# Adding the two halves of a feature block by a transfer instead of by VectorE, in a decoder trunk on one core

## The chip, the cores and the metric

The kernel runs on one core of a Trainium2 chip. The metric is the device time of one execution in microseconds (us). A core has engines that work side by side, each in the order of its own queue: TensorE (PE in the profile, with its weight loads as PEld), VectorE (DVE), ScalarE (ACT), GpSimd (POOL) and SyncE (SP). Transfers are issued from a queue of SP, ACT or POOL and are then moved by 16 DMA engines. An instruction whose input is not there yet holds up everything behind it in its queue.

## The reference

The reference is a decoder trunk of two layers on 256 tokens of width 2048. Each layer is a mixer and then a squared-ReLU MLP, with norms ahead of them and residual sums behind them. The change touches the MLP alone:

```
def squared_relu_mlp(h, w1, w2):
    return jnp.square(jax.nn.relu(h @ w1)) @ w2
...
        x = x + mix
        x = x + squared_relu_mlp(rms_norm(x, norm_mlp[layer]), mlp_w1[layer], mlp_w2[layer])
```

Here `w1` is 2048 x 8192 and `w2` is 8192 x 2048, both in float32.

## The kernel before, in words

**Split numbers.** Every weight tile is loaded as float32 (`load`, line 127, issued from SP, four buffers) and split in two parts (`halves`): ScalarE writes the rounded part `wh` (line 135), VectorE writes the rest, `wl`, as the difference (line 136). A product is then a sum of three (or two) TensorE products of parts. A raw buffer comes free, and SP can issue the next load into it, when its readers on both engines are done.

**Feature blocks.** An MLP runs in four quarters q. A quarter makes 16 blocks of 128 hidden features each. In a block (`steps_feats` with `bank=3`, `mm_feats`) TensorE multiplies the 16 weight tiles of the block with the tokens' tile, whose 512 columns are 256 tokens of the high part and 256 of the low part (line 164), and adds the product of `wl` and the high part to the first 256 columns (line 168). So the PSUM tile `h` has two halves that must be added. All these blocks use one PSUM bank: the next block's first matmul waits until ScalarE has copied the bank out.

**Evacuation.** `evac_h` does it, once per block: ScalarE copies the bank to `bt_h` (line 1027), VectorE adds the halves into `hu` (line 1029), ScalarE takes the ReLU (line 1030) and the square (line 1032 or 1041). For 12 blocks of a quarter (`SEVEN` = 6 pairs) every second block then makes four sums out of the pair's `hp` on VectorE (lines 1043 to 1045) and splits them into `pt` on ScalarE and VectorE (lines 1047, 1048). The other four blocks are split into `ht`.

**What runs between blocks.** The second product (`steps_seven`) is done for pairs by seven products in place of eight. Each pair has a `go_a` and a `go_b`; they load two tiles `wr`, make their sums `ta` and `tb` on VectorE (lines 225 to 228) and split all of these. `woven` puts 12 such steps between 8 blocks. I call 8 blocks with the steps between them a stretch: a quarter has one for its blocks 0 to 7 (steps on the columns 1024 on, of the quarter before) and one for its blocks 8 to 15 (steps on the columns 0 on). Blocks 0 to 7 of the first quarter stand apart and are not woven.

**What sets the order.** The Python order of calls is only the input of a scheduler: it puts each engine's instructions into a queue by data dependences and its own idea of when each is ready, and an instruction may stand in its queue ahead of one that was written earlier. The order shown below is what came out.

Of the kernel before, what the change touches and what calls it, by code (L numbers as in the profile page):

```python
# [9 lines left out]
F32 = mybir.dt.float32  # L10
FR = mybir.dt.float32r
AF = mybir.ActivationFunctionType
OP = mybir.AluOpType

P = 128
S = 256
# [53 lines left out]
def trunk(ctx: ExitStack, tc: tile.TileContext, plan, a, c_first, c_even, c_odd, out):  # L70
    nc = tc.nc
# [23 lines left out]
    def acc(name, bank=None):  # L95

        if bank is None:
            bank = n_a[0] % 4
            n_a[0] += 1
        return pacc.tile([P, 512], F32, name=name, tag=f"acc{bank}", bufs=1)  # L100
# [70 lines left out]
    def steps_tokens(Ts, w, c0, n, evac, kt=2, order=None, name="a", split_first=False):  # L171

        order = list(order if order is not None else range(len(Ts)))
        box = {}
        groups = [order[i:i + kt] for i in range(0, len(order), kt)]
        if split_first:
            groups[:1] = [[k] for k in groups[0]]

        def make(gi, g):
            def go():  # L180
                if gi == 0:
                    box["a"] = [acc(f"{name}{b}") for b in range(NB)]
                hi, lo = weights(w, g[0], len(g), c0, n)
                for j, k in enumerate(g):
                    mm_tokens(box["a"], n, Ts[k], hi[:, j, :], lo[:, j, :],
                              gi == 0 and j == 0, gi == len(groups) - 1 and j == len(g) - 1)
                if gi == len(groups) - 1:
                    evac(box["a"])
            return go

        return [make(gi, g) for gi, g in enumerate(groups)]
# [239 lines left out]
    def weave(main, side):  # L431

        done = 0
        for i, go in enumerate(main):
            go()
            want = (i + 1) * len(side) // max(1, len(main))
            while done < want:
                side[done]()
                done += 1
        for go in side[done:]:  # L440
            go()
# [509 lines left out]
    def finish(H, wq, evac_y, scale, sm):  # L951

        gfs = []
        for i, (o, n, tag, bufs) in enumerate(((0, 1024, "hp", 1), (1024, 512, "bt", 2), (1536, 512, "bt", 2))):
            g = sm.tile([P, n], F32, name=f"gf{i}", tag=tag, bufs=bufs)
            nc.gpsimd.dma_start(g, a["norm_final"][o:o + n].rearrange("(o d) -> o d", o=1).to_broadcast([P, n]))
            gfs.append((o, n, g))

        def gf(lo, hi):
            return next(g[:, lo - o:hi - o] for o, n, g in gfs if o <= lo < o + n)  # L960

        ss = [sm.tile([P, 5], F32, name=f"ss_f{b}") for b in range(NB)]

        def stats(b, i, v):
            nc.scalar.activation(junk[:, :v.shape[-1]], v, AF.Square, accum_out=ss[b][:, i:i + 1])

        def gain(c):
            def go():
                for b in range(NB):
                    nc.vector.tensor_mul(x[b][c], x[b][c], gf(c * 512, (c + 1) * 512))  # L970
            return go

        for c in range(2):
            for b in range(NB):
                stats(b, c, x[b][c])
        weave(steps_tokens(Late(H), wq, 1024, 512, evac_y(2), name="y"), [gain(0), gain(1)])
        for b in range(NB):
            stats(b, 2, x[b][2])

        def add(b, o, ac):  # L980
            nc.vector.scalar_tensor_tensor(x[b][3][:, o:o + 256], ac[:, :256], scale["s"][:, b:b + 1],
                                           x[b][3][:, o:o + 256], OP.mult, OP.add)

        def evac_a(ac):
            for b in range(NB):
                add(b, 0, ac[b])
                stats(b, 3, x[b][3][:, 0:256])
                nc.vector.tensor_mul(x[b][3][:, 0:256], x[b][3][:, 0:256], gf(1536, 1792))

        weave(steps_tokens(Late(H), wq, 1536, 256, evac_a, kt=4, name="y"), [gain(2)])  # L990
        w = [weights(wq, k, 4, 1792, 256) for k in range(0, 16, 4)]
        for b in range(NB):
            ac = acc(f"z{b}")
            for k in range(16):
                hi, lo = (t[:, k % 4, :] for t in w[k // 4])
                mm_three(ac[:, :256], operand(H[k], b), (hi, lo), k == 0, k == 15)
            add(b, 256, ac)
            stats(b, 4, x[b][3][:, 256:])
            t = sm.tile([P, 3], F32, name=f"var_f{b}")
            nc.vector.tensor_reduce(t[:, 0:1], ss[b], mybir.AxisListType.X, OP.add)  # L1000
            nc.vector.tensor_scalar(t[:, 1:2], t[:, 0:1], 1.0 / D, EPS, OP.mult, OP.add)
            nc.gpsimd.tensor_tensor(t[:, 2:3], t[:, 1:2], neg_half[:, :1], OP.pow)
            r = t[:, 2:3]
            rows = slice(b * P, (b + 1) * P)
            for c in (0, 1):
                nc.vector.tensor_scalar(x[b][c], x[b][c], r, None, OP.mult)
                nc.sync.dma_start(out[0, rows, c * 512:(c + 1) * 512], x[b][c])
            nc.vector.scalar_tensor_tensor(x[b][3][:, 256:], x[b][3][:, 256:], r, gf(1792, 2048), OP.mult, OP.mult)
            nc.scalar.activation(x[b][2], x[b][2], AF.Copy, scale=r)
            nc.sync.dma_start(out[0, rows, 1024:1536], x[b][2])  # L1010
            nc.scalar.activation(x[b][3][:, 0:256], x[b][3][:, 0:256], AF.Copy, scale=r)
            nc.sync.dma_start(out[0, rows, 1536:2048], x[b][3])

    def mlp(layer, norm, nxt):
        st = ExitStack()
        sm = st.enter_context(tc.tile_pool(name=f"mlp{layer}", bufs=1))
        X = Late(norm.T)
        scale = {}
        NF = FF // NQ // P

        def evac_h(H):
            def make(c):
                box = {}

                def go(f, ac):
                    t = sm.tile([P, 512], F32, name="bt_h", tag="bt", bufs=2)
                    nc.scalar.activation(t, ac, AF.Copy)
                    u = sm.tile([P, S], F32, name="hu", tag="hu", bufs=2)
                    nc.vector.tensor_add(u, t[:, :S], t[:, S:])  # L1029
                    nc.scalar.activation(u, u, AF.Relu)  # L1030
                    if c >= SEVEN:
                        nc.scalar.activation(u, u, AF.Square)
                        H[2 * c + f] = sm.tile([P, 2, S], FR, name="ht", tag="ht", bufs=2 * (NF // 2 - SEVEN))
                        split_to(H[2 * c + f], u)
                        return
                    if f == 0:
                        box["r"] = sm.tile([P, 8, P], F32, name="hp", tag="hp", bufs=1)
                    r = box["r"]
                    dst = r[:, 1:3, :] if f == 0 else r[:, 0:4:3, :]
                    v = u.rearrange("p (b t) -> p b t", b=NB)  # L1040
                    nc.scalar.activation(dst, v, AF.Square)
                    if f == 1:
                        nc.vector.tensor_tensor(r[:, 4:6, :], r[:, 1:3, :], r[:, 2:4, :], OP.subtract)
                        nc.vector.tensor_tensor(r[:, 6, :], r[:, 5, :], r[:, 1, :], OP.subtract)
                        nc.vector.tensor_tensor(r[:, 7, :], r[:, 0, :], r[:, 6, :], OP.add)
                        pt = sm.tile([P, 2, 8, P], FR, name="pt", tag="pt", bufs=SEVEN)
                        nc.scalar.activation(pt[:, 0], r, AF.Copy)
                        nc.vector.tensor_tensor(pt[:, 1], r, pt[:, 0].bitcast(F32), OP.subtract)
                        H[2 * c], H[2 * c + 1] = (pt, 0), (pt, 1)
                return go  # L1050
            return make
# [32 lines left out]

        def blocks(q, H):

            ev = evac_h(H)

            def block(i):
                def go():  # L1090
                    run(steps_feats(X, ("mlp_w1", layer, 0), q * (FF // NQ) + i * P,
                                    lambda f, ac: ev[i // 2](i % 2, ac), n=P, name="h", kt=8, bank=3))
                return go

            ev = [ev(c) for c in range(NF // 2)]
            return [block(i) for i in range(NF)], ev

        H = [None] * NF
        hs, ev = blocks(0, H)
# [8 lines left out]
        for q in range(NQ):  # L1108
# [16 lines left out]
            H = [None] * NF  # L1125
# [11 lines left out]
    mix, w_out, ev, side, st = even_layer(n0)  # L1137
# [5 lines left out]
    mix, w_out, ev, side, st = odd_layer(n2)  # L1143
# [53 lines left out]
```

## Time and profile before

| what | us |
|---|---|
| three runs | 2128.31, 2131.53, 2126.43 (median 2128.31) |
| the profiled execution's own time | 2125.81 |
| its span, first to last instruction | 2124.0 |
| TensorE busy | 2098.3 |
| VectorE busy | 1727.1 |
| ScalarE busy | 1301.9 |
| GpSimd busy | 6.1 |

TensorE is busy for 99% of the span. Its matmuls are pipelined and their shown durations overlap, so the gaps before its instructions say more than the share: a row of the timeline ends with the idle time of the engine just before the row, and what ended it. The first MLP runs from about 359 to 1050 us, the second from about 1428 to 2112 us.

### The profile page before, as it was taken

The numbers are of one execution on the slowest core, as the hardware profiler recorded it, in microseconds if no ns is written. First come the engines' busy times: TensorE is split into PE (matmuls) and PEld (weight loads), VectorE is DVE, ScalarE is ACT, GpSimd is POOL, SyncE is SP. The second block draws the span as 40 slices with busy tenths as digits, with TensorE's granted clock in tenths as the row PEclk, the third lists the DMA queues.
The fourth block names the chain that finished last, engine by engine and source line by source line (L and its number), as shares of the span: only waits on it lengthen the run. The fifth ranks groups of instructions, "written<-read, shape, count | busy, mean of one in ns | idle before, by whom it ended". The sixth has DMA issues, their size and how long they took to land.

```text
span 2124.0 us, 29506 instructions
## 1 busy us (share of the span) xinstructions
PE 2098.3 (99%) x10953; PEld 1803.9 (85%) x10953; DVE 1727.1 (81%) x2432; ACT 1301.9 (61%) x1871; POOL 6.1 (0%) x13
## 2 busy tenths in 40 slices
PE   9999999999999999999999999999999999999998
PEld 8998888888888888888888888888888888888887
DVE  5678555889999999899877667558899999998985
ACT  6675445766676666667544444557666666666663
POOL 0000000000000000000000000000000000000000
PEclk9999999999999999999999999999999999999999
DMA  8554455556566566565655555555665665665664
GB/s 294 168 175 157 159 178 179 189 185 212 180 210 195 193 199 205 187 211 190 201 190 172 177 177 169 166 182 179 200 195 189 208 198 189 207 197 193 205 216 141
DMA packets 115296, 404.51 MB, mean 190 GB/s; under 512 B 12944, under 2 KB 13584, under 8 KB 115152
## 3 DMA queue, kind: packets, MB, share of 16 engines
q1 hardware_dynamic: 114624, 401.07, 58.0%
q0 software_dynamic: 384, 1.51, 0.3%
q8 instruction: 85, 1.39, 0.3%
q14 instruction: 59, 0.48, 0.1%
q10 hardware_dynamic: 144, 0.06, 0.0%
HBM read 400.49 MB, written 2.10 MB: 190 GB/s over the span
## 4 chain that ended last, share of the span: by engine, by line
PE 67%; DVE 19%; DMA 8%; issue 3%; ACT 2%; DVEq 0%; POOLq 0%; POOL 0%; SPq 0%; ACTq 0%
PE h L164 12%; DVE wl L136 11%; DMA wr<-in_mlp_w 8%; PE h L168 6%; PE k L164 3%; PE o L154 3%; PE o L156 3%; PE o L155 3%; PE q L164 3%; PE yc L154 3%; PE yc L155 3%; PE yc L156 3%; DVE ta L225 2%; PE v L154 2%; PE v L156 2%
## 5 line engine op out<-in xcount | busy, mean ns | idle before, releaser
L136 DVE TENSOR_TENSOR wl<-wr,wh 128x1024 fp32r<-128x1024 f32 (+4 forms) x769 | 865.8, 1136 | 270.4 <-ACT wh L135 264.9
L135 ACT ACTIVATE wh<-wr 128x1024 fp32r<-128x1024 f32 (+4 forms) x769 | 752.7, 987 | 512.9 <-PE h L164 121.0
L164 PE MATMUL h<-T,wh 128*128 128x512 f32 x2048 | 515.1, 392 | 9.9 <-ACT wh L135 7.8
L164 PEld LDWEIGHTS h<-T,wh 128*128 128x128 f32 x2048 | 373.9, 188 | 90.1 <-ACT wh L135 11.6
L168 PEld LDWEIGHTS h<-T,wl 128*128 128x128 f32 x2048 | 279.3, 190 | 20.1
L168 PE MATMUL h<-T,wl 128*128 128x256 f32 x2048 | 285.5, 282 | 0.0
L225 DVE TENSOR_TENSOR ta<-wr,wr 128x1024 f32<-128x1024 f32 x87 | 106.3, 1222 | 46.4 <-DMA wr<-in_mlp_w 46.0
L155 PE MATMUL ym<-wl,pt 128*128 128x512 f32 x348 | 136.7, 393 | 0.0
L156 PE MATMUL ym<-wh,pt 128*128 128x512 f32 x348 | 135.4, 389 | 0.0
L154 PE MATMUL ym<-wh,pt 128*128 128x512 f32 x348 | 135.4, 392 | 0.0
L135 ACT ACTIVATE wh<-ta 128x1024 fp32r<-128x1024 f32 x87 | 92.1, 1059 | 61.4 <-DVE ta L225 60.1
L1030 ACT ACTIVATE hu<-hu 128x256 f32<-128x256 f32 x128 | 52.8, 416 | 106.4 <-DVE hu L1029 106.3
L135 ACT ACTIVATE wh<-tb 128x1024 fp32r<-128x1024 f32 x87 | 91.8, 1056 | 34.2 <-DVE tb L228 34.2
L154 PE MATMUL yc<-wh,pt 128*128 128x512 f32 x285 | 111.3, 390 | 0.0
L155 PE MATMUL yc<-wl,pt 128*128 128x512 f32 x285 | 111.2, 390 | 0.0
L156 PE MATMUL yc<-wh,pt 128*128 128x512 f32 x285 | 110.9, 389 | 0.0
L136 DVE TENSOR_TENSOR wl<-tb,wh 128x1024 fp32r<-128x1024 f32 x87 | 106.1, 1220 | 3.8 <-ACT wh L135 3.3
L136 DVE TENSOR_TENSOR wl<-ta,wh 128x1024 fp32r<-128x1024 f32 x87 | 106.0, 1218 | 0.0
L154 PE MATMUL o<-wh,M 128*128 128x512 f32 x256 | 102.3, 400 | 0.0
L156 PE MATMUL o<-wh,M 128*128 128x512 f32 x256 | 99.8, 390 | 0.0
L155 PE MATMUL o<-wl,M 128*128 128x512 f32 x256 | 99.6, 389 | 0.0
L154 PE MATMUL yc<-wh,ht 128*128 128x512 f32 x240 | 93.6, 390 | 0.0
(314 smaller groups left out, 3405.3 us busy)
## 6 DMA issues: line engine op xcount, KB each, us to landing
wr<-in_mlp_w SPq DMA_DIRECT2D x512, 512.0 KB, 4.1
wr<-in_od_w_qkv SPq DMA_DIRECT2D x96, 512.0 KB, 4.1
wr<-in_ev_w_in SPq DMA_DIRECT2D x32, 512.0 KB, 3.5
wr<-in_ev_w_out SPq DMA_DIRECT2D x32, 512.0 KB, 3.5
wr<-in_od_w_out SPq DMA_DIRECT2D x32, 512.0 KB, 3.4
wr<-in_ev_w_in SPq DMA_DIRECT2D x24, 344.0 KB, 3.0
wr<-in_ev_w_in SPq DMA_DIRECT2D x15, 364.0 KB, 5.8
wr<-in_mla_w_ukv SPq DMA_DIRECT2D x8, 512.0 KB, 3.6
```

Source lines behind the costliest of these rows:

```text
L135: nc.scalar.activation(hi, raw, AF.Copy)
L136: nc.vector.tensor_tensor(lo, raw, hi.bitcast(F32), OP.subtract)
L154: nc.tensor.matmul(ac, xh, hi, start=first, stop=False)
L155: nc.tensor.matmul(ac, xh, lo, start=False, stop=False)
L156: nc.tensor.matmul(ac, xl, hi, start=False, stop=last)
L164: nc.tensor.matmul(acs[f], hi[:, j, f * P:(f + 1) * P], Ts[j].rearrange("p a t -> p (a t)"), start=first and j == 0, stop=False)
L168: nc.tensor.matmul(acs[f][:, :S], lo[:, j, f * P:(f + 1) * P], Ts[j][:, 0, :], start=False, stop=last and j == n - 1)
L225: nc.vector.tensor_tensor(ta, r0, r1[:, 0:1, :].to_broadcast([P, 2, 512]), OP.add)
L1030: nc.scalar.activation(u, u, AF.Relu)
```

## The change

The tile of the copied bank now takes the sum too: the two halves are added into its first 256 columns. In 12 of 16 blocks of a quarter (those with `i % 8 < 6`; in the first quarter only blocks 8 to 13) the sum is made by a transfer from SBUF to SBUF that adds to its destination and is issued from POOL. In the other blocks VectorE makes it, as before. The rest of a block's evacuation (`rest`: ReLU, square, sums, splits) is kept in `held` and called in the evacuation of the next block, behind that block's copy and add; where VectorE made the sum it is called at once. The tag `bt` has three buffers of 512 columns in place of two, and the tag `hu` (two of 256) is gone.

```
-        def evac_h(H):
+        held = []
+
+        def evac_h(H, by_dma):
             def make(c):
                 box = {}
 
                 def go(f, ac):
-                    t = sm.tile([P, 512], F32, name="bt_h", tag="bt", bufs=2)
-                    nc.scalar.activation(t, ac, AF.Copy)
-                    u = sm.tile([P, S], F32, name="hu", tag="hu", bufs=2)
-                    nc.vector.tensor_add(u, t[:, :S], t[:, S:])
+                    u = sm.tile([P, 512], F32, name="bt_h", tag="bt", bufs=3)
+                    nc.scalar.activation(u, ac, AF.Copy)
+                    if 2 * c + f in by_dma:
+                        nc.gpsimd.dma_start(u[:, :S], u[:, S:], accum_op=OP.add)
+                    else:
+                        nc.vector.tensor_add(u[:, :S], u[:, :S], u[:, S:])
+                    for g in held:
+                        g()
+                    held[:] = [lambda: rest(f, u[:, :S])]
+                    if 2 * c + f not in by_dma:
+                        held.pop()()
+
+                def rest(f, u):
                     nc.scalar.activation(u, u, AF.Relu)
...
-            ev = evac_h(H)
+            ev = evac_h(H, [i for i in range(NF) if i % 8 < 6 and (q or i >= 8)])
```

In ScalarE's queue before, where the first MLP's third quarter begins (blocks 0 and 1; L1027 is the copy of the bank, L1030 the ReLU, L1041 the square, L135 a weight's rounded part):

```order
L1027 ACTIVATE bt_h_6525<-h0_6480 128x512
L1030 ACTIVATE hu_6527<-hu_6527 128x256
L1041 ACTIVATE hp_6530<-hu_6527 128x256
L135 ACTIVATE wh562_6641<-wr559_6635 128x1024
L135 ACTIVATE wh563_6646<-ta561_6639 128x1024
L135 ACTIVATE wh565_6656<-wr560_6637 128x512
L1027 ACTIVATE bt_h_6611<-h0_6566 128x512
L135 ACTIVATE wh564_6652<-tb561_6640 128x1024
L1030 ACTIVATE hu_6613<-hu_6613 128x256
L1041 ACTIVATE hp_6530<-hu_6613 128x2x128
```

The same place in ScalarE's queue now (L1031 is the copy, L1043 the ReLU, L1054 the square, L1060 the split of `hp`):

```order
L1031 ACTIVATE bt_h_6493<-h0_6448 128x512
L1043 ACTIVATE bt_h_6493<-bt_h_6493 128x256
L135 ACTIVATE wh562_6599<-wr559_6593 128x1024
L1054 ACTIVATE hp_6579<-bt_h_6493 128x256
L135 ACTIVATE wh563_6604<-ta561_6597 128x1024
L135 ACTIVATE wh564_6610<-tb561_6598 128x1024
L135 ACTIVATE wh565_6614<-wr560_6595 128x512
L1031 ACTIVATE bt_h_6575<-h0_6530 128x512
L135 ACTIVATE wh567_6630<-wr566_6628 128x1024
L135 ACTIVATE wh569_6652<-wr568_6650 128x1024
L1043 ACTIVATE bt_h_6575<-bt_h_6575 128x256
L1054 ACTIVATE hp_6579<-bt_h_6575 128x2x128
```

Although `rest` is called a block later, the ReLU of a block stands right behind the copy of its own block, or behind two splits of weights, and not behind the copy of the next block.

In ScalarE's queue before, at the blocks 3 and 4 of the same stretch:

```order
L1027 ACTIVATE bt_h_6778<-h0_6733 128x512
L1030 ACTIVATE hu_6780<-hu_6780 128x256
L1041 ACTIVATE hp_6719<-hu_6780 128x2x128
L135 ACTIVATE wh589_6899<-ta587_6892 128x1024
L135 ACTIVATE wh588_6894<-wr585_6888 128x1024
L1047 ACTIVATE pt_6787<-hp_6719 128x1024
L135 ACTIVATE wh590_6905<-tb587_6893 128x1024
L135 ACTIVATE wh591_6909<-wr586_6890 128x512
L135 ACTIVATE wh593_6925<-wr592_6923 128x1024
L135 ACTIVATE wh595_6947<-wr594_6945 128x1024
L1027 ACTIVATE bt_h_6881<-h0_6836 128x512
```

The same place in ScalarE's queue now:

```order
L1031 ACTIVATE bt_h_6740<-h0_6695 128x512
L135 ACTIVATE wh589_6859<-ta587_6852 128x1024
L1043 ACTIVATE bt_h_6740<-bt_h_6740 128x256
L1054 ACTIVATE hp_6744<-bt_h_6740 128x2x128
L135 ACTIVATE wh588_6854<-wr585_6848 128x1024
L135 ACTIVATE wh590_6865<-tb587_6853 128x1024
L135 ACTIVATE wh591_6869<-wr586_6850 128x512
L135 ACTIVATE wh593_6885<-wr592_6883 128x1024
L1060 ACTIVATE pt_6845<-hp_6744 128x1024
L135 ACTIVATE wh595_6907<-wr594_6905 128x1024
L1031 ACTIVATE bt_h_6837<-h0_6792 128x512
```

One split of a weight (wh589) has moved ahead of the ReLU; all others stand behind it. Of the 84 blocks whose halves a transfer adds, 8 have no split between copy and ReLU, 33 have one, 35 two and 8 three.

## Rows read from the trace of the kernel before

**Rows 1.** The page: the span, and each engine's busy time, share and instructions.
```profile
span 2124.0 us, 29506 instructions
...
PE 2098.3 (99%) x10953; PEld 1803.9 (85%) x10953; DVE 1727.1 (81%) x2432; ACT 1301.9 (61%) x1871; POOL 6.1 (0%) x13
```
**Rows 2.** A 50-us window, busy us (instructions): PE, PEld, DVE, ACT, POOL; clock, DMA share, GB/s.
```profile
700.00:750.00 50.00, 48.66 (x243) 40.72 (x242) 47.90 (x62) 32.88 (x42) 0.00 (x0) 1.00 0.54 180
```
**Rows 3.** Waits of TensorE's matmuls, whole span: us in total, times, longest.
```profile
PE h L164 <- ACT wh L135: 7.8, 9, 1.4
...
PE h L164 <- ACT bt_h L1027: 1.9, 6, 0.4
```
**Rows 4.** Groups by line and shape: count, busy us, mean ns, idle before.
```profile
L135 ACT ACTIVATE wh<-wr 128x1024 fp32r<-128x1024 f32 x629 | 661.4, 1056 | 454.3 <-PE h L164 115.0 <-PE o L156 71.8 <-issue 62.1
...
L1027 ACT ACTIVATE bt_h<-h 128x512 f32<-128x512 f32 x128 | 73.8, 583 | 6.1 <-PE h L168 6.1
...
L135 ACT ACTIVATE wh<-wr 128x512 fp32r<-128x512 f32 x91 | 56.8, 624 | 34.3 <-PE yc L156 13.8 <-DMA wr<-in_mlp_w 9.1 <-PE h L164 5.9
...
L1029 DVE TENSOR_TENSOR hu<-bt_h 128x256 f32<-128x256 f32 x128 | 53.0, 419 | 2.3 <-ACT bt_h L1027 2.2
L1030 ACT ACTIVATE hu<-hu 128x256 f32<-128x256 f32 x128 | 52.8, 416 | 106.4 <-DVE hu L1029 106.3
L1047 ACT ACTIVATE pt<-hp 128x1024 fp32r<-128x1024 f32 x48 | 50.7, 1056 | 12.0 <-DVE hp L1045 12.0
...
L1041 ACT ACTIVATE hp<-hu 128x256 f32<-128x256 f32 x96 | 38.9, 411 | 1.8
```
**Rows 5.** The timeline of ScalarE in a stretch of the third quarter: start, us, instruction, idle.
```profile
669.18 0.58 ACT L1027 ACTIVATE bt_h<-h 128x512 f32<-128x512 f32 x1
...
676.19 0.60 ACT L1027 ACTIVATE bt_h<-h 128x512 f32<-128x512 f32 x1 [0.32 <-PE h L168]
...
697.93 0.42 ACT L1030 ACTIVATE hu<-hu 128x256 f32<-128x256 f32 x1 [1.85 <-DVE hu L1029]
...
700.67 1.06 ACT L135 ACTIVATE wh<-ta 128x1024 fp32r<-128x1024 f32 x1 [1.88 <-DVE ta L225]
...
704.59 2.51 ACT L135 ACTIVATE wh<-wr 128x512 fp32r<-128x512 f32 x3
707.01 0.57 ACT L1027 ACTIVATE bt_h<-h 128x512 f32<-128x512 f32 x1
```
**Rows 6.** The timeline of TensorE in the same stretch.
```profile
707.63 2.14 PE L164 MATMUL h<-T,wh 128*128 128x512 f32 x8 [0.42 <-ACT bt_h L1027]
...
719.21 2.14 PE L164 MATMUL h<-T,wh 128*128 128x512 f32 x8 [0.93 <-ACT wh L135]
```
**Rows 7.** The timeline of VectorE: the sums of a pair.
```profile
679.42 0.42 DVE L1043 TENSOR_TENSOR hp<-hp 128x256 f32<-128x256 f32 x1
679.87 0.29 DVE L1044 TENSOR_TENSOR hp<-hp 128x128 f32<-128x128 f32 x1
```
**Rows 8.** DMA issues: queue, count, KB each, median us from issue to landing.
```profile
wr<-in_mlp_w SPq DMA_DIRECT2D x512, 512.0 KB, 4.1
...
out<-x SPq DMA_DIRECT2D x8, 256.0 KB, 2.7
...
gf<-in_norm_final POOLq DMA_DIRECT2D x2, 256.0 KB, 5.1
...
x<-in_x_t SPq DMA_DIRECT2D x2, 128.0 KB, 3.1
```
**Rows 9.** The tile gf, loaded by three transfers from POOL's queue.
```profile
L956 POOL DMA_DIRECT2D gf<-in_norm_final x3: 536/536/583, 2031.5 to 2061.3; - x3
...
DMA to landing us min/median/max: 4.5/5.5/5.7
```
**Rows 10.** The chain that ended last, 655 to 725 us: loads on it.
```profile
667.89 4.34 DMA wr<-in_mlp_w
...
707.75 3.50 DMA wr<-in_mlp_w
```

More of the change, by code (lines that the diff above doesn't have):

```diff
@@ L953, in finish @@
         gfs = []
-        for i, (o, n, tag, bufs) in enumerate(((0, 1024, "hp", 1), (1024, 512, "bt", 2), (1536, 512, "bt", 2))):
+        for i, (o, n, tag, bufs) in enumerate(((0, 1024, "hp", 1), (1024, 512, "bt", 3), (1536, 512, "bt", 3))):
             g = sm.tile([P, n], F32, name=f"gf{i}", tag=tag, bufs=bufs)
```

## The prediction

> **What bounds the kernel now.** I read the page first: TensorE is busy for 2098.3 of 2124.0 us [rows 1]. That share is no room by itself, so I went to the waits of TensorE: in the feature blocks of the MLPs its matmuls waited 7.8 us for rounded weights from ScalarE and 1.9 us for the PSUM bank that ScalarE copies out, 9.7 us together [rows 3]. This is all that the change can give back there. Then the busy time inside an MLP: in 50 us VectorE is busy for 47.9 and ScalarE for 32.9 [rows 2]. VectorE is nearly as full as TensorE, ScalarE has 17 us in 50 free. Last, the timelines of one stretch. The bank's next user, the first matmul of block 5, waited 0.42 us for the copy of block 4, and block 6 waited 0.93 us for a rounded weight [rows 6]; the copy of block 4 itself began only at 707.01, behind splits that had waited 1.88 us for a sum of VectorE, and behind a ReLU that had waited 1.85 us for the add of the halves [rows 5]. So TensorE sets the time, and ScalarE and VectorE are only just in time at the end of a stretch. A delay of ScalarE of more than a microsecond or two late in a stretch is a stop of TensorE.
>
> **What is removed.** Of 128 adds on VectorE, at 419 ns each [rows 4], 84 go (6 in each of 14 stretches): 84 x 0.419 = 35.2 us of busy time, 2.5 us in a stretch. ScalarE's wait for the add goes with them: 106.3 us over 128 ReLUs [rows 4], 0.83 us each. Neither is on TensorE's path but through the 9.7 us above, so the gain is at most 9.7 us, and I book all of it, since a stop by the new wait stands in the place of the old stops.
>
> **What is added.** 84 transfers of 128 KB from POOL's queue, and 84 waits of a ReLU on ScalarE for them. POOL has 6.1 us of work in all [rows 1], so the issue, 0.54 us for a transfer of this queue [rows 9], costs none of the other engines anything; only the last two of them stand behind the first load of `gf`, which waits for the last reader of a buffer. I cost that at nothing, since ScalarE's splits cover a wait of a microsecond there, and at most at one more landing, about 4 us, if they don't.
>
> Call L the time from the end of the copy to the sum being in place. No row of before has an adding transfer, so I bound L: the quickest landing of any large transfer is 2.7 us (256 KB, from SP's queue), the slowest of POOL's queue 5.7 us [rows 8, 9]. Two rows are near: 128 KB from SP's queue, the right size, 3.1 us, and 256 KB from POOL's queue, the right queue, 5.1 us [rows 8]. I take their middle, 4.1 us. The ends 2.7 and 5.7 are kept for the range.
>
> **What stands behind the wait.** In its queue the ReLU stands behind the copy of its own block with none to three splits between, not behind the next block's copy. While it waits, the rounded weights behind it are not made, nor is the next copy, and TensorE waits for both. VectorE then has only the work whose inputs are already there.
>
> I follow ScalarE from the copy of block 0 to that of block 4, with the durations of [rows 4]: copy 0.58, ReLU 0.42, square 0.41, a weight split 1.06 (or 0.62 for a half tile), a `pt` split 1.06. What stands between a ReLU and the next copy, and so cannot overlap the transfer: block 0, ReLU, square, three splits and a half one, copy, 5.2 us; block 1, ReLU, square, the three sums of VectorE (0.42, 0.29 and 0.29 us [rows 7] for the last two of one shape), `pt`, two splits, copy, 5.6 us; block 2 as block 0, 5.2 us; block 3, ReLU, square, four splits and a half one, `pt`, copy, 7.3 us. That is 23.3 us. ScalarE's instructions overlap a little: half, whole and whole split are 2.74 us by their means, and the next instruction began 2.42 us after their start [rows 5], so at the least it is 0.9 times as much, 21 us. I take 22.2 us.
>
> The copy of block 0 ended at 669.18 + 0.58 = 669.76, and block 5 could have begun at 707.63 - 0.42 = 707.21 [rows 5, 6]. That leaves 37.45 us for four landings and 22.2 us of work: (37.45 - 22.2) / 4 = 3.81 us. Up to L = 3.8 us TensorE sees nothing. Beyond it, four waits in a row add up, as nothing between them gives time back, and TensorE stops for S = 4 x (L - 3.81) us in a stretch. Blocks 6 and 7 keep the add on VectorE, and there ScalarE catches up, so I count each of the 14 stretches for itself. At L = 4.1 us, S is 1.2 us, and 14 x 1.2 = 16.2 us.
>
> **The sum.** -9.7 + 16.2 = +6.5 us on the profiled execution's 2125.81 us: 2132.3 us. The runs' median, 2128.31, is 2.5 us above that execution, so I forecast 2134.8, rounded 2135 us. It is a narrow balance: the two terms meet at L = 3.98 us, and each 0.1 us of L is 5.6 us.
>
> **A rule of the skill.** The trace has POOL's transfers landing 4.5 to 5.7 us after their issue, for 256 and 512 KB [rows 9]. The Trainium skill's page "DMA: Bandwidth & Descriptors", section "Anatomy of one DMA — SWDGE (gpsimd) path", gives such a transfer a fixed cost of about 2.0 us and 436 KB per further microsecond; for 128 KB that is an estimate of 2.3 us, and for the 256 KB of the trace 2.6 us where the rows have 5.1. By the rule L would be under 3.8 us and the first rival below would hold; the trace's queue, beside the weights' loads, does not bear it out.
>
> **Rivals.**
> 1. *The landing is hidden.* If L is under about 3.8 us (all rows of before load from or store to HBM, and a transfer inside SBUF may be quicker, which speaks for it; the slow rows of POOL's queue speak against it), no stop is added, and VectorE's 2.5 us a stretch shorten what came late there. Half of the 9.7 us comes back, 2125.8 - 4.9 + 2.5 = 2123.4 us; all of it would be 2118.6. Chance 0.38, of which some is within the bound of no change, since the square and the splits now stand behind a split that waits for `ta`.
> 2. *The waits add up badly.* The same chain as the forecast, but with L as POOL's own rows have it, 5.1 us: S = 5.2 us, 14 x 5.2 = 72 us, less 9.7: 2125.8 + 62.5 + 2.5 = 2191 us. It decides from L = 4.8 us on. An adding transfer also has to read its destination, which speaks for it. Chance 0.15.
> 3. *The loads are late.* The weights' loads lie on the chain that ended last, four of them in 70 us, of 3.5 to 5.2 us [rows 10], the first and the last of the four. An adding transfer moves a quarter of a load's 512 KB, by its 4.1 us [rows 8] about 1.0 us of the engines. If two of the four loads in a stretch are each held up by it, 14 x 2 = 28 us, less the 9.7: 2125.8 + 18.3 + 2.5 = 2146.6 us, slower, whatever L is. Against it: the DMA engines have a share of 0.54 only [rows 2]. Chance 0.10.
>
> **How the numbers follow.** The forecast with L between about 3.8 and 4.8 us has 0.37. What a measurement can tell from no change is 0.2%, 4.3 us. Slower by more: rivals 2 and 3, and of the forecast's cases those above L = 4.06 us, some 0.22: together 0.47. Faster by more: most of rival 1, 0.30. No change gets the rest, 0.23. The range: below it ends a little under the case in which all 9.7 us come back (2118.6), at 2117; above it goes to L = 4.8 us, S = 4.0 us, 14 x 4.0 - 9.7 = 46 us, 2125.8 + 46 + 2.5 = 2174 us. The likeliest case alone spans 2119 to 2174 as well, as its L does; the end at L = 5.7 us (S = 7.6 us, +97 us) is left out.
>
> **What would show it.** In the profile after: 84 fewer adds on VectorE and some 35 us less busy time there; 84 transfers on POOL's queue whose median landing is 4 us or a little less, counted from the issue; ScalarE's ReLU waiting for that transfer 1 to 3 us in most blocks (0.83 us before); and TensorE waiting in the feature blocks for the copy of the bank (L1031) and for `wh`, about 16 us in place of 9.7, most of it at blocks 4 to 6 of a stretch. I am wrong if the transfers land in under 3.5 us and these waits of TensorE shrink, or if TensorE stops for the loads of weights instead.

## The result, and the profile after

The changed kernel takes 2232.01 us (median, 2228.53 to 2239.33) beside 2128.82 us of the kernel before on the same chip: 1.0493 times as long, 95% interval 1.0475 to 1.0511. The prediction said 2135 us with a range to 2174. Slower was right; the size, 103 us in place of 6.5, was not.

The page's first lines, to lay beside [rows 1]:

```profile
span 2237.6 us, 29744 instructions
PE 2142.7 (96%) x10953; PEld 1813.2 (81%) x10953; DVE 1710.2 (76%) x2348; ACT 1282.7 (57%) x1871; POOL 79.0 (4%) x97
```

TensorE is busy for 96% of the span in place of 99%, and its busy time itself grew by 44 us with the same number of matmuls. TensorE's waits, after [rows 3] (engine, line that waited, releaser: total us, times, longest):

```profile
PE h L164 <- ACT bt_h L1031: 37.5, 21, 2.9
PE ym L155 <- DVE wl L136: 20.5, 31, 1.0
PE h L164 <- ACT wh L135: 10.4, 12, 2.1
PE ym L154 <- ACT wh L135: 5.6, 9, 0.7
...
PE yc L155 <- DVE wl L136: 4.2, 9, 0.7
```

They are 78.2 us in 82 stops where the prediction had 9.7 us to lose or win. In the feature blocks (the rows of `h`, 47.9 us) most of it, 37.5 us, is for the PSUM bank, which ScalarE copies out late; the rows of `ym` and `yc` are the second product's waits for parts of weights. ScalarE's groups by line and shape, after [rows 4], show why:

```profile
L135 ACT ACTIVATE wh<-ta 128x1024 fp32r<-128x1024 f32 x87 | 91.9, 1057 | 119.0 <-DVE ta L225 118.8
L1031 ACT ACTIVATE bt_h<-h 128x512 f32<-128x512 f32 x128 | 73.1, 578 | 0.0
L1043 ACT ACTIVATE bt_h<-bt_h 128x256 f32<-128x256 f32 x128 | 52.9, 417 | 258.8 <-DMA bt_h<-bt_h 207.9 <-DVE bt_h L1035 50.8
```

The ReLU (L1043) waited 207.9 us for the transfers, and 106.3 us for VectorE's adds before [rows 4]. The transfers on POOL's queue, and their landing beside that of the weights' loads (KB each, median us from issue to landing), answer to [rows 8]:

```profile
wr<-in_mlp_w SPq DMA_DIRECT2D x512, 512.0 KB, 4.3
bt_h<-bt_h POOLq DMA_DIRECT2D x84, 128.0 KB, 5.2
```

In ScalarE's timeline the first block of a stretch looks like this; its place in the kernel before is the first row of [rows 5] (start, us, what, idle before):

```profile
692.56 1.05 ACT L135 ACTIVATE wh<-wr 128x1024 fp32r<-128x1024 f32 x1
693.52 0.58 ACT L1031 ACTIVATE bt_h<-h 128x512 f32<-128x512 f32 x1
699.25 0.42 ACT L1043 ACTIVATE bt_h<-bt_h 128x256 f32<-128x256 f32 x1 [5.16 <-DMA bt_h<-bt_h]
699.57 1.04 ACT L135 ACTIVATE wh<-wr 128x1024 fp32r<-128x1024 f32 x1
```

Copy and ReLU are neighbours in the queue, so ScalarE does nothing for the whole landing, 5.15 us from the copy's end. That is one of the quicker landings at this place: over the 14 first blocks the mean is 6.3 us. What that does to TensorE, and to its clock, is best seen late in another stretch. TensorE's timeline around the copy of block 4:

```profile
829.45 0.39 PE L156 MATMUL ym<-wh,pt 128*128 128x512 f32 x1
832.57 3.20 PE L164 MATMUL h<-T,wh 128*128 128x512 f32 x8 [2.73 <-ACT bt_h L1031]
835.57 1.62 PE L168 MATMUL h<-T,wl 128*128 128x256 f32 x8
837.02 1.98 PE L164 MATMUL h<-T,wh 128*128 128x512 f32 x8
```

And the same time in windows of 2 us (mind the numbers behind POOL: granted clock, share of the DMA engines, GB/s):

```profile
828.00:830.00 2.00, 1.84 (x9) 1.16 (x7) 2.00 (x5) 0.93 (x1) 0.00 (x0) 1.00 0.71 215
830.00:832.00 2.00, 0.00 (x0) 0.00 (x0) 1.95 (x2) 1.97 (x3) 0.00 (x0) 1.00 0.71 217
832.00:834.00 2.00, 1.43 (x5) 1.14 (x6) 1.86 (x3) 0.52 (x2) 0.87 (x1) 0.82 0.83 270
834.00:836.00 2.00, 2.00 (x8) 1.62 (x7) 1.93 (x3) 1.06 (x1) 0.00 (x0) 0.50 0.98 202
836.00:838.00 2.00, 2.00 (x12) 1.84 (x12) 1.43 (x2) 0.00 (x0) 0.00 (x0) 0.83 0.64 218
```

TensorE stood for 2.73 us; then the granted clock fell to 0.50, the lower of its two levels, and eight matmuls took 3.20 us where eight alike took 1.98 us a moment later. The mean granted clock of the span is 0.989, of before 0.999: 0.011 x 2237.6 - 0.001 x 2124.0 = 22 us of full-speed work not done, or a little less, since TensorE also stood for parts of the slow stretches.

Earlier in the same stretch the clock fell behind shorter stops: there TensorE's listed waits were of 0.74 and 0.78 us, with TensorE busy for 0.96 of 2 us in the window ahead:

```profile
796.00:798.00 2.00, 0.96 (x3) 0.48 (x3) 2.00 (x3) 1.28 (x3) 0.42 (x1) 1.00 0.00 0
798.00:800.00 2.00, 1.61 (x5) 1.01 (x5) 1.53 (x3) 1.03 (x2) 0.45 (x1) 0.79 0.69 212
800.00:802.00 2.00, 1.24 (x3) 0.83 (x3) 1.94 (x2) 1.97 (x4) 0.00 (x0) 0.50 1.05 281
```

So of the profiled span's growth of 113.6 us, 68.5 us are TensorE's listed waits (78.2 less 9.7). A stop costs more than its row lists: from 829.45 to 832.57 there are 3.12 us, of which a matmul needs 0.23 us, so 2.89 us were lost where the row lists 2.73 us. Counted in this way from start to start, the 82 stops cost 93.2 us, and the 15 before cost 12.1 us for their 9.7: another 12.6 us. Matmuls at the lower clock outside these stops took 19 us more, and the rest, some 12 us, lies in gaps too short for the list, most of them ahead of `ym` and `yc`.

### The profile page after: what moved, and what is told of

Same layout as the page of the kernel before. It is cut to its first block, busy times and chain, and to the rows that moved or that the text cites. A ratio compares the mean times of both kernels' runs of the same rounds, so it can differ in the third digit from the quotient of the medians.

```text
span 2237.6 us, 29744 instructions
## 1 busy us (share of the span) xinstructions
PE 2142.7 (96%) x10953; PEld 1813.2 (81%) x10953; DVE 1710.2 (76%) x2348; ACT 1282.7 (57%) x1871; POOL 79.0 (4%) x97
## 3 DMA queue, kind: packets, MB, share of 16 engines
q0 software_dynamic: 12480, 12.52, 3.5%
## 4 chain that ended last, share of the span: by engine, by line
PE 42%; issue 41%; DMA 8%; DVE 4%; ACT 3%; POOL 2%; POOLq 0%; DVEq 0%; ACTq 0%; SPq 0%
DMA bt_h<-bt_h 7%; PE h L164 3%; PE k L164 3%; PE o L156 3%; PE o L154 3%; PE o L155 3%; PE q L164 3%; PE v L154 2%; PE v L156 2%; PE v L155 2%; POOL bt_h L1033 2%; ACT wh L135 2%; DVE wl L136 2%; PE h L168 2%; PE k L168 1%
## 5 line engine op out<-in xcount | busy, mean ns | idle before, releaser
L135 ACT ACTIVATE wh<-wr 128x1024 fp32r<-128x1024 f32 (+4 forms) x769 | 749.4, 984 | 410.9 <-PE o L156 71.8
L164 PE MATMUL h<-T,wh 128*128 128x512 f32 x2048 | 529.8, 401 | 48.0 <-ACT bt_h L1031 37.5
L164 PEld LDWEIGHTS h<-T,wh 128*128 128x128 f32 x2048 | 379.6, 192 | 138.7 <-ACT bt_h L1031 48.5
L168 PEld LDWEIGHTS h<-T,wl 128*128 128x128 f32 x2048 | 284.6, 194 | 21.1
L1043 ACT ACTIVATE bt_h<-bt_h 128x256 f32<-128x256 f32 x128 | 52.9, 417 | 258.8 <-DMA bt_h<-bt_h 207.9
L155 PE MATMUL ym<-wl,pt 128*128 128x512 f32 x348 | 142.1, 408 | 20.6 <-DVE wl L136 20.5
L135 ACT ACTIVATE wh<-ta 128x1024 fp32r<-128x1024 f32 x87 | 91.9, 1057 | 119.0 <-DVE ta L225 118.8
L225 DVE TENSOR_TENSOR ta<-wr,wr 128x1024 f32<-128x1024 f32 x87 | 106.4, 1223 | 46.9 <-DMA wr<-in_mlp_w 46.6
L1033 POOL DMA_DIRECT2D bt_h<-bt_h x84 | 73.0, 869 | 1936.1 <-ACT bt_h L1031 1491.9
L135 ACT ACTIVATE wh<-tb 128x1024 fp32r<-128x1024 f32 x87 | 91.5, 1052 | 45.9 <-DVE tb L228 45.9
L155 PEld LDWEIGHTS ym<-wl,pt 128*128 128x128 f32 x348 | 65.9, 189 | 46.3 <-DVE wl L136 37.3
```

Of the source, the lines that this page charges most:

```text
L135: nc.scalar.activation(hi, raw, AF.Copy)
L155: nc.tensor.matmul(ac, xh, lo, start=False, stop=False)
L164: nc.tensor.matmul(acs[f], hi[:, j, f * P:(f + 1) * P], Ts[j].rearrange("p a t -> p (a t)"), start=first and j == 0, stop=False)
L168: nc.tensor.matmul(acs[f][:, :S], lo[:, j, f * P:(f + 1) * P], Ts[j][:, 0, :], start=False, stop=last and j == n - 1)
L225: nc.vector.tensor_tensor(ta, r0, r1[:, 0:1, :].to_broadcast([P, 2, 512]), OP.add)
L1033: nc.gpsimd.dma_start(u[:, :S], u[:, S:], accum_op=OP.add)
```

## The experiments

Each was timed beside the kernel before on one chip: 2129.11 us for the first four, 2128.61 for the next four, 2128.78 for the last three. A stretch is 8 blocks, 14 stretches have transfers, and the diffs are against the changed kernel unless said otherwise.

**The rest of the evacuation really behind the next block's copy.**

```
-                    nc.scalar.activation(u, ac, AF.Copy)
+                    copy = nc.scalar.activation(u, ac, AF.Copy)
...
                     for g in held:
-                        g()
+                        with tc.issue_after(copy.ins):
+                            g()
```

> As after, but the ReLU of a block whose halves a transfer adds is really queued behind the next block's copy on ScalarE (an order edge, no other edit). Theory A (the loss is ScalarE standing at the ReLU for a landing of 5.2 us with weight splits and the next copy behind it): the next copy comes 7 to 10 us later, so the landing is hidden; ScalarE's wait for these transfers falls from 208 to under 20 us, TensorE's waits in the feature blocks from 48 to 12 us or less, TensorE's clock stays at its full level, time 2117 to 2135 us. Theory B (the transfers hold up the loads of weights, or the chip's transfers cost time wherever the ReLU stands): TensorE or VectorE still waits for loads, 2155 us or more.

Measured: 2138.11 us, 1.0044 [1.0029, 1.0059]. The 84 transfers are as before (landing 5.2 us), no ReLU waits for one, and 94 of the 103 us are gone. What is left of TensorE's waits has nothing in a feature block:

```profile
PE ym L155 <- DVE wl L136: 10.4, 11, 1.8
PE ym L154 <- ACT wh L135: 7.3, 7, 1.7
```

So nearly all of the loss is the place of the ReLU in ScalarE's queue, not the transfers' traffic. But the kernel is still 9 us slower than before, just above what I expected.

**Transfers that nobody waits for.** VectorE adds the halves in every block, the rest is called at once, and the transfers go into a scratch tile, set to zero once, that is not read.

```
-                        nc.gpsimd.dma_start(u[:, :S], u[:, S:], accum_op=OP.add)
-                    else:
-                        nc.vector.tensor_add(u[:, :S], u[:, :S], u[:, S:])
+                        nc.gpsimd.dma_start(junk[:, S:], u[:, S:], accum_op=OP.add)
+                    nc.vector.tensor_add(u[:, :S], u[:, :S], u[:, S:])
...
-                    if 2 * c + f not in by_dma:
-                        held.pop()()
+                    held.pop()()
```

> VectorE adds the halves in all blocks, in place, and ScalarE's ReLU follows at once as in the kernel before; beside it the same 84 adding transfers of 128 KB run from POOL, into a tile that nobody reads. Theory A: 2122 to 2140 us, transfers landing in about 5 us without anybody waiting. Theory B (the transfers themselves cost the time, through the loads of weights): 2150 to 2230 us, weight loads landing clearly later than 4.1 us.

Measured: 2136.55 us, 1.0030 [1.0017, 1.0043]: by the ratio the transfers alone cost 6.4 us (3.6 to 9.2). VectorE's group of `ta` (busy us, mean ns, idle before) shows where:

```profile
L225 DVE TENSOR_TENSOR ta<-wr,wr 128x1024 f32<-128x1024 f32 x87 | 106.4, 1224 | 64.7 <-DMA wr<-in_mlp_w 64.6
```

It waited 64.6 us for loads of weights, and 46.0 us in the kernel before.

**Without the adds.** This one is the kernel before; in the 84 blocks the ReLU reads the first half alone, so the product with the low part of the tokens is left out there.

```
-                    nc.vector.tensor_add(u, t[:, :S], t[:, S:])
-                    nc.scalar.activation(u, u, AF.Relu)
+                    if 2 * c + f in chosen:
+                        nc.scalar.activation(u, t[:, :S], AF.Relu)
+                    else:
+                        nc.vector.tensor_add(u, t[:, :S], t[:, S:])
+                        nc.scalar.activation(u, u, AF.Relu)
```

> The kernel before, with the add of the halves left out in the same 84 blocks (the ReLU reads the first half alone, so the product of the tokens' low part is missing there). It shows what VectorE's relief is worth when nothing takes its place. Theory A: TensorE sets the time and waits only 9.7 us, so 2118 to 2129 us. Rival (VectorE bounds the MLPs): its 35 us come back, 2094 us.

Measured: 2125.14 us, 0.9984 [0.9974, 0.9993]. By the ratio, all that the removal of 84 adds can give is about 3.4 us (1.5 to 5.5).

**Every second transfer.** Blocks 0, 2 and 4 of a stretch, 42 transfers.

```
-            ev = evac_h(H, [i for i in range(NF) if i % 8 < 6 and (q or i >= 8)])
+            ev = evac_h(H, [i for i in range(NF) if i % 8 in (0, 2, 4) and (q or i >= 8)])
```

> As after, but only every second of these blocks (the 1st, 3rd and 5th of a stretch) has a transfer, 42 in all; VectorE adds the others. Theory A with waits that add up along a stretch: between the copies of blocks 0 and 4 two landings of 5.2 us and two waits of 0.83 us stand beside 22.2 us of work, 34.3 of the 37.45 us there, so TensorE hardly stops: 2119 to 2140 us. Rival (each transfer costs the same by itself, 103 us over 84): 2129 + 42 x 1.23 = 2180 us.

Measured: 2215.16 us, 1.0395 [1.0373, 1.0418]. Both numbers fell: half the transfers keep 83% of the loss (86 of 103 us). That broke the prediction's chain, in which two landings would have drawn on the room of four, and made me look at single blocks. In the table, "growth" is worked out from ScalarE's timeline: the time from the start of one block's copy to the next one's, less the same in the kernel before, summed over the 14 stretches (a copy that is moved in its queue shows with opposite signs in two neighbours). "Wait" is the idle time of the ReLU of that block for its transfer, summed likewise.

| us, sums over 14 stretches | 0→1 | 1→2 | 2→3 | 3→4 | 4→5 | 5→6 | 6→7 |
|---|---|---|---|---|---|---|---|
| one interval before, mean | 7.3 | 10.4 | 8.7 | 10.7 | 8.3 | 9.9 | 8.3 |
| changed kernel: splits ahead of the ReLU | 0 or 1 | 2 or 3 | 2 | 1 | 1 (once 2) | 2 | - |
| changed kernel: wait | 80.9 | 15.2 | 17.2 | 20.3 | 22.7 | 51.6 | - |
| changed kernel: growth | 45.4 | -2.6 | 10.2 | 36.1 | 16.1 | 7.0 | -15.3 |
| every second: wait | 80.2 | - | 4.8 | - | 89.8 | - | - |
| every second: growth | 44.3 | -1.2 | 4.9 | 4.4 | 43.9 | -6.4 | 0.0 |
| only block 0: wait | 80.8 | - | - | - | - | - | - |
| only block 0: growth | 46.2 | 0.3 | 10.0 | 2.8 | -1.9 | 2.9 | -0.4 |
| blocks 1 and 2: wait | - | 28.5 | 16.2 | - | - | - | - |
| blocks 1 and 2: growth | 0.3 | 6.6 | 5.7 | -5.1 | 6.5 | -4.6 | -0.1 |
| block 0 held back: wait | 0.4 | 15.7 | 14.8 | 14.7 | 23.8 | 51.3 | - |
| block 0 held back: growth | 4.0 | -1.9 | 5.4 | 35.3 | 17.0 | 8.4 | -19.1 |
| 0, 3 and 4 held back: growth | 2.9 | -2.1 | 4.6 | -8.8 | 28.6 | 2.7 | -12.5 |

With every second block, the growth stands at 0→1 and 4→5 alone: the two blocks whose ReLU comes right behind the copy, or at block 0 in 6 of 14 cases behind one split. Block 2, with two splits between, waits and loses next to nothing. My new theory was that each block has a room of its own.

**Only block 0 of a stretch**, 14 transfers (`i % 8 == 0` in the same line).

> Only block 0 of each of the 14 stretches is summed by a transfer; its ReLU stands right behind its copy (8 of 14) or behind one split (6 of 14). If each landing that no split covers stops TensorE by itself (28 such waits cost 86 us in the kernel with every second block, 3.1 us each), 14 of them cost 35 to 45 us: about 2165 us, 2155 to 2178, with TensorE waiting at block 1 of a stretch for the copy of block 0 or for wh. If waits matter only when four of them add up over a stretch (the chain of the prediction), one of 5 us is far under the 15 us of room: 2122 to 2134 us. If each transfer costs the same wherever it is (86 us over 42), 14 cost 29: about 2157 us.

Measured: 2190.35 us, 1.0294 [1.0277, 1.0311]. 14 transfers cost 62 us, 4.4 us each, more than any theory had. The additive chain (2122 to 2134) is refuted: one wait of 5.8 us in a stretch is not swallowed by the 15 us of room that the sum saw. TensorE stops later than expected: of its 36.7 us of waits in the feature blocks 22.1 us come before block 2 and 11.3 us before block 6. The windows of the stretch with the second longest wait (7.31 us) show something else as well:

```profile
688.00:690.00 2.00, 2.00 (x14) 1.78 (x13) 1.75 (x2) 0.00 (x0) 0.00 (x0) 1.00 1.02 316
690.00:692.00 2.00, 2.00 (x15) 1.79 (x14) 0.86 (x2) 0.00 (x0) 0.00 (x0) 1.00 0.20 68
692.00:694.00 2.00, 2.00 (x10) 1.68 (x9) 0.01 (x1) 1.41 (x3) 0.00 (x0) 1.00 0.04 17
694.00:696.00 2.00, 1.38 (x6) 0.67 (x5) 1.97 (x2) 2.00 (x3) 0.00 (x0) 1.00 0.00 0
```

ScalarE waited here until 692.59. VectorE ran out of rounded weights, SP waited 8.0 us for VectorE to free a raw buffer and issued no load from 686.8 to 695.25, and from 690 to 696 us the DMA engines were nearly idle. The loads behind them come later for it: the wait stops the weights' loads too.

**Only blocks 1 and 2**, 28 transfers, with two or three splits between copy and ReLU (`i % 8 in (1, 2)`).

> Blocks 1 and 2 of each stretch are summed by a transfer, 28 in all; between the copy and its ReLU stand three splits (14 times) or two (14 times). If only uncovered landings cost, ScalarE's waits for the transfers are under 25 us together and the time is 2126 to 2136 us (28 transfers' own cost of about 2 us, less a little of VectorE's relief). If each transfer costs the same wherever it is (2.05 us), 28 cost 57: about 2186 us. The chain of the prediction gives 2122 to 2134 us here as well.

Measured: 2135.26 us, 1.0039 [1.0025, 1.0052]. Twice the transfers of the last run, and a tenth to an eighth of its cost. The ReLU's idle time there:

```profile
  DVE bt_h L1035: 109.0, 90
  DMA bt_h<-bt_h: 44.7, 24
```

44.7 us of waits, more than the 25 expected, cost 6.7 us by the medians (8.3 by the ratio), traffic included; 80.8 us at block 0 cost 62. It isn't the number of transfers nor the sum of the waits, but the block in which a wait falls.

**The rest called at once**, with the transfers (`held.pop()()` without its `if`).

> As the changed kernel, but the rest of the evacuation is called at once and not a block later. If the deferral does nothing, because the scheduler puts the ReLU back behind the copy of its own block anyway (here with 0, 1 or 2 splits between in 10, 45 and 29 of 84 blocks, there 0 to 3 in 8, 33, 35 and 8), the time is the changed kernel's or a little more: 2225 to 2260 us. If the deferral as it stands hides a good part of the landings, its absence costs at least 40 us more: 2270 us or above.

Measured: 2266.51 us, 1.0659 [1.0640, 1.0677], between the two expectations. The deferral as the scheduler took it is worth 34 us, though no ReLU stands behind the next copy: the one of block 5, for instance, waited 69.7 us without it and 51.6 us with it.

**The deferral alone.** VectorE adds in every block, and the rest of the 84 stands behind the next copy.

```
-                    nc.scalar.activation(u, ac, AF.Copy)
-                    if 2 * c + f in by_dma:
-                        nc.gpsimd.dma_start(u[:, :S], u[:, S:], accum_op=OP.add)
-                    else:
-                        nc.vector.tensor_add(u[:, :S], u[:, :S], u[:, S:])
+                    copy = nc.scalar.activation(u, ac, AF.Copy)
+                    nc.vector.tensor_add(u[:, :S], u[:, :S], u[:, S:])
                     for g in held:
-                        g()
+                        with tc.issue_after(copy.ins):
+                            g()
```

> No transfers: VectorE adds the halves in every block; the ReLU of the 84 blocks stands behind the next block's copy (held there). If the 10 us that remained in the kernel with the same order and the transfers come from the transfers' load on the DMA engines, this one is not slower than before: 2118 to 2129 us, since ScalarE no longer waits 0.83 us for each add. If they come from the deferral (the pair's sums and splits come a block later), it stays at about 2134 to 2140 us.

Measured: 2130.08 us, 1.0010 [1.0001, 1.0020], a microsecond above the first range. Deferring alone costs about 2 us, at most 4, and gains nothing: the 0.83 us that ScalarE waited per add were already hidden. The other 7 of the first experiment's 9 us are about the traffic's 6.4; `ta` waited 64.2 us for loads there.

**Block 0 alone held behind the next copy.**

```
                     for g in held:
-                        g()
+                        if (2 * c + f - 1) % 8 == 0:
+                            with tc.issue_after(copy.ins):
+                                g()
+                        else:
+                            g()
```

> As the changed kernel, but the ReLU of block 0 of each stretch really stands behind the copy of block 1 (14 of the 84; the others stand where they stood, with one to three splits in front). In the changed kernel the way from copy to copy has grown, over 14 stretches, by 45 us from block 0 to 1, by 36 from 3 to 4 and by 16 from 4 to 5. If each block has only its own room, and block 0 the least, those 45 us go and nothing else does: about 2187 us, 2176 to 2198. If four waits draw on one pool of 15 us in a stretch (the chain of the prediction), three landings of 5.15 us fit into it: 2128 to 2145 us. If a fixed half of ScalarE's wait is lost (208 us of waits for 104), 81 us of wait go with block 0: about 2192 us.

Measured: 2194.15 us, 1.0310 [1.0293, 1.0327]: 38 us gone. In the table the growth at 0→1 falls from 45.4 to 4.0 and 3→4, 4→5 keep 35.3 and 17.0. With three landings left the pooled chain would have had next to no loss. This run doesn't tell "own room" from "half of each wait"; the 28 transfers at blocks 1 and 2 do.

**Blocks 0, 3 and 4 held back** (`in (0, 3, 4)` in that condition).

> As before, but the ReLUs of blocks 0, 3 and 4 stand behind the next copy (42 of 84); blocks 1, 2 and 5 stay behind their own copies with two to four splits in front. If each block has its own room, 45 + 36 + 16 us go: 2132 to 2150 us, with at most 10 us more of TensorE's waits than in the kernel with all 84 held back (2138). If a fixed half of ScalarE's wait is lost, 124 us of 208 go: about 2170 us. The pooled chain gives 2128 to 2140 us here.

Measured: 2154.81 us, 1.0132 [1.0108, 1.0155], between the two expectations. 3→4 and 4→5 together fall from 52 to 20 us and no further. ScalarE's longest waits there are for something else:

```profile
ACT wh L135 <- DVE ta L225: 147.3, 66, 5.4
...
ACT bt_h L1047 <- DMA bt_h<-bt_h: 66.0, 41, 4.1
```

147.3 us for `ta`, more than twice the 63.1 of the kernel before, and VectorE's `ta` itself waited 71.9 us for loads (46.0 before). Which order of ScalarE's queue makes these loads late was not tried.

**A quarter of the bytes.** The transfers that nobody waits for, with 64 of 256 columns.

```
-                        nc.gpsimd.dma_start(junk[:, S:], u[:, S:], accum_op=OP.add)
+                        nc.gpsimd.dma_start(junk[:, S:S + 64], u[:, S:S + 64], accum_op=OP.add)
```

> VectorE adds the halves in all blocks and nobody waits for the 84 transfers, as in the run in which they cost 6.4 us; here each moves 64 of the 256 columns (32 KB in place of 128 KB, as many rows). If their bytes on the DMA engines delay the weights' loads, a quarter of the cost stays, 1.6 us: 2126 to 2132 us, and VectorE's wait for loads at ta falls from 64.6 us towards the 46.0 of the kernel before. If the number of transfers or of their packets does it, the time stays at 2133 to 2139 us.

Measured: 2130.15 us, 1.0006 [0.9997, 1.0016], where the full size had 1.0030.

```profile
L225 DVE TENSOR_TENSOR ta<-wr,wr 128x1024 f32<-128x1024 f32 x87 | 106.3, 1222 | 48.8 <-DMA wr<-in_mlp_w 48.5
```

As many transfers with as many packets (12480 on their queue in both pages), and the wait of `ta` is back at 48.5 us: the bytes delay the loads, about 6.4 us for 84 x 128 KB. The removed adds are worth about 3.4 us, so a version with all 84 transfers has little to win even if nobody waits for them; no run here was faster than the kernel before with transfers in it.

## Why the prediction was wrong

**The step that failed** is the one room for four blocks: "Up to L = 3.8 us TensorE sees nothing. Beyond it, four waits in a row add up", out of 37.45 us less 22.2 us of work. It let block 0 borrow from blocks 1 to 3. A block cannot, or hardly: TensorE soon needs the rounded weights behind the ReLU (with block 0 alone it stops before block 2), and the raw buffers for the next loads come free behind them too. Block by block, worked out after the result, with the prediction's own work (5.2 us from block 0's ReLU to the next copy, at its 0.95): before, copy 0 to copy 1 takes 7.3 us in the mean, so the room is 7.3 - 4.9 = 2.4 us; the wait was 80.9 / 14 = 5.8 us; 14 x 3.4 = 48 us are lost, and the growth was 45.4. With every second block, 4→5 has 8.3 - 4.9 = 3.4 us of room, a wait of 6.4, 14 x 3.0 = 42 us; measured 43.9. At 3→4 the ReLU's wait (20.3 us) hides what the landing costs: the split that stands ahead of it there is the one of `ta`, and it waits itself, 47.1 us over the 14 blocks (21.5 before), although `ta` is ready no later than before (3.3 us after the copy's end, 3.7 before). ScalarE used to fill that time with the ReLU and the square. Now 5.9 us pass from the copy's end to the ReLU, for one split done; with the prediction's 7.3 x 0.95 = 6.9 us of work behind it, less 10.7, 14 x 2.1 = 29 us are lost, and `pt` waits another 10.4 us for VectorE's sums; measured 36.1. The room of block 0 could have been read beforehand: in the timeline of before its interval is the shortest of the stretch, and in the order now the ReLU stands right behind the copy there.

**L was too small**: 4.1 us taken, while from the copy's end to the landing it was 6.3, 4.4, 4.4 and 5.8 us in the mean at blocks 0 to 3, 5.2 us over the four. It depends on the place, and the slowest landings (8.0 us from the issue) lay beyond the upper bound of 5.7. With 5.2 us the prediction's own formula gives 14 x 5.6 - 9.7 = +69 us, not far from rival 2's +62.5. That is near the growth of TensorE's listed waits, 68.5 us, but by luck: the same formula gives no loss for the 14 transfers that cost 62. The estimate of 2.3 us from the Trainium skill ("DMA: Bandwidth & Descriptors", "Anatomy of one DMA — SWDGE (gpsimd) path") was further off still.

**The clock was not in the sum.** About 20 us, a fifth of the loss, came from stretches at the lower level behind stops. The kernel before was at its full clock up to its last 4 us, so its trace did not show this.

**Traffic was booked at nothing** in the forecast and at two late loads per stretch in rival 3 (28 us): it is 6.4 us where nobody waits for the transfers, by late loads of `ta`'s weights. In the changed kernel itself `ta` waited 46.6 us for loads, as long as before (46.0), so what part of its loss is traffic is not shown.

**The gain was about 3.4 us**, not 9.7. VectorE's busy time fell by 16.9 us, not 35; with the ReLUs behind the next copy it fell by 28 (to 1698.8 us), 0.34 us an add, since the shown durations of neighbours overlap.

**What held**: the ReLU stands behind its own block's copy and waits there; in the feature blocks TensorE waits mostly for the bank, and mostly late in a stretch (29.2 of 47.9 us before block 5), though holding back block 0 alone gave back 38 us. Late loads explain little of the loss, as their chance of 0.10 had it.

## What to carry to other kernels

Price a new wait in an in-order queue at the one place where it stands: the interval between its neighbours in the trace, less the work that cannot move ahead of it, was all the room there was here, and the rooms of later steps could not be borrowed, with TensorE waiting right behind. Count from where the landing begins: an instruction ahead of the wait that itself waits for something covers little. Before adding a deferral, read in the built order whether it is there: written a block later, it was scheduled back, and one explicit "issue after" took away 94 of 103 us. And a transfer that relieves an engine pays in bytes on the DMA engines that feed that engine, here about 6.4 us for a relief of about 3.4.

## What the runs showed of the hardware

- After a stop of TensorE of 2.73 us its granted clock was 0.82, 0.50 and 0.83 in the next three windows of 2 us, while it was busy, and eight matmuls took 3.20 us in place of 1.98; a stop cost more than its length. Elsewhere it fell behind listed stops of 0.74 and 0.78 us, with TensorE busy for half of the 2 us ahead.
- An SBUF-to-SBUF transfer of 128 KB that adds to its destination landed in 5.2 us (median) beside the weights' loads, longer than a load of 512 KB (4.3 us). It depends on the place: 5.9 us at the first block of a stretch (6.2 us where these 14 were the only ones), 4.2 and 4.4 us at the next two. With nobody waiting it was 4.9 us, with 32 KB each 4.3 us.
- Its issue took POOL 869 ns each, against 536 for a plain load of that queue [rows 9]:

```profile
L1033 POOL DMA_DIRECT2D bt_h<-bt_h x84 | 73.0, 869 | 1936.1 <-ACT bt_h L1031 1491.9 <-DVE wl L136 393.7 <-DVE tb L228 40.6
```
